# Merge-gate projections in pairs: seven products of half the size for eight, with their sums made ahead

## The chip, the cores and the metric

The kernel is one program on one core of a Trainium2 chip. The metric is device time in microseconds; before the change it is 1770.51 us, the median of 3 runs (1770.02 to 1771.18).

## What is computed

Two layers of a hybrid encoder on 512 tokens of width 1024. Each layer normalises its input to `h`, makes all queries, keys, values and gates by one projection `h @ w_in`, runs three attentions, and merges their outputs `u_a`, `u_b`, `u_m` (each already multiplied by its own gate) like this:

```python
y_a = u_a @ w_br_diff;  y_b = u_b @ w_br_dil;  y_m = u_m @ w_br_mem
gates = sigmoid(h @ w_in[:, mgate])            # 3 x 1024 columns
merged = gates[0] * y_a + gates[1] * y_b + gates[2] * y_m
x = x + merged @ w_out
```

The change touches `h @ w_in[:, mgate]`, a product of 512x1024 by 1024x3072 in each layer, and the operand of the last line.

## The kernel before

**Precision.** Every large product is made in float32r from two parts of each operand, `hi` (rounded by ScalarE, L95) and `lo = src - hi` (VectorE, L96; both in `split`, L94). `mm3` (L166) then issues three matmuls on TensorE: hi by hi (L167), hi by lo (L168), lo by hi (L169).

**Weights.** `weight_order` (L99) lists all weight units in the order of their use, most of 1024x128 (a tile of 128 partitions by 8x128). `weight` (L159) calls `prefetch` (L148), which keeps two units ahead (`LEAD`): it loads a unit from HBM on SyncE's queue into one of 3 raw buffers and splits it into one of 4 `w_hi` and one of 3 `w_lo` buffers.

**Projections.** `proj_fm` (L171) makes 128 output channels for all 512 tokens: the weight's 128x128 blocks are stationary, the transposed activations `hT_hi` and `hT_lo` (8 blocks of 128x512, made once a layer by `norm_T`, L320) move. It is 8 blocks by `mm3`, 24 matmuls of 512 columns, summed in one of four PSUM banks named `mm`.

**A layer.** First the memory keys and values and `hT`, then the attentions, which the generators in `weave` (L657) interleave, then `merge` (L580). `merge` makes 16 gated tiles `U`, read back from DRAM and split, then goes over 8 slices `d` of 128 output channels. A slice is three `proj_fm` for its gates with a sigmoid each (L601 to L603), `y` (48 matmuls with `u` moving, from the weight units `ba` and `bm`, L605 to L613), and on VectorE three products and two sums (L615 to L617) and a split into `mg_hi`, `mg_lo`. `out_proj` (L624) then holds blocks of `mg` stationary and moves `w_out` in 512 columns; it feeds the next layer's `norm_T`, or the final norm.

**Order.** Each engine works in its own order; a scheduler places instructions on the engines from the program's order and its own estimates. GpSimd (POOL) only prepares the bias tables at the start of the program.

Of the kernel before, what the change touches and what calls it, by code (L numbers as in the profile page):

```python
# [44 lines left out]
def encoder_kernel(ctx: ExitStack, tc: tile.TileContext, x, mem, g_norm, w_in, diff_lambda,  # L45
                   w_mem_kv, g_mem, w_br_diff, w_br_dil, w_br_mem, w_out, rel_bias, g_final,
                   buckets, maskrows, partrows, out):
    nc = tc.nc
# [50 lines left out]
    def weight_order():  # L99
# [19 lines left out]
        for l in range(DEPTH):  # L119
# [15 lines left out]
            for d in range(8):  # L135
                ds_ = slice(d * 128, (d + 1) * 128)
                for b in range(3):
                    yield fm(l, MGATE + b * 1024 + d * 128)
                yield ("ba", l, d), 8, 128, [(0, 8, 0, 128, w_br_diff[l, :, ds_])]
                yield ("bm", l, d), 8, 128, [(0, 4, 0, 128, w_br_mem[l, :, ds_]),  # L140
                                             (4, 8, 0, 128, w_br_dil[l, :, ds_])]
# [683 lines left out]
```

## Time and profile before

| | |
|---|---|
| median of 3 runs | 1770.51 us |
| the profiled execution | 1770.44 us, its span 1768.4 us |
| mean granted TensorE clock | 0.998 |
| busy share of the span | PE 99%, DVE 57%, ACT 47%, POOL 1% |
| matmul instructions | 9012 |
| chain that ended last | PE 97%, DMA 1%, ACT 1% |

The span is the program on the core; the 2 us over it are launch and end. PE is TensorE's matmuls, PEld its weight loads, DVE VectorE, ACT ScalarE, POOL GpSimd, SP the SyncE queue that issues most transfers. Matmuls are pipelined, so that the duration shown for one is longer than the distance to the next: what one costs a full engine is read from the starts of neighbours.

### The profile page before, as it was taken

How to read it: one execution, taken by the hardware profiler on the slowest of the kernel's cores; microseconds unless marked ns; L12 is line 12 of the kernel's file. 1: busy time of each engine (PE TensorE's matmuls, PEld its weight loads, DVE VectorE, ACT ScalarE, POOL GpSimd, SP SyncE). 2: the span in 40 equal slices, each digit the busy share in tenths (PEclk: the TensorE clock that was granted, in tenths of full speed). 3: DMA queues.
4: the chain of work that ended last, by engine and by line, in shares of the span. 5: the costliest groups of instructions: out<-in, count | busy, mean ns of one | idle time of the engine just before them, and what ended most of it. 6: DMA issues, size and time to landing. Idle time of an engine off the chain costs nothing.

```text
span 1768.4 us, 23429 instructions
## 1 busy us (share of the span) xinstructions
PE 1743.8 (99%) x9012; PEld 1496.0 (85%) x9012; DVE 1005.5 (57%) x1727; ACT 834.5 (47%) x1436; POOL 22.1 (1%) x45
## 2 busy tenths in 40 slices
PE   7999999999999999999999999999999999999998
PEld 6798889888888888888888898888988888888886
DVE  6566576666765663333465656658566747333333
ACT  6455555545555642222255555455454548322223
POOL 2200000000000000000000000000000000000000
PEclk9999999999999999999999999999999999999999
DMA  9643243332432643333572333324332336333342
GB/s 263 141 130 86 72 123 89 103 94 76 117 97 80 202 138 95 97 93 116 160 199 59 112 85 103 94 76 116 95 98 86 101 109 202 107 96 95 96 154 72
DMA packets 308847, 200.26 MB, mean 113 GB/s; under 512 B 14116, under 2 KB 283428, under 8 KB 308736
## 3 DMA queue, kind: packets, MB, share of 16 engines
q1 hardware_dynamic: 306704, 195.09, 38.3%
q0 software_dynamic: 2032, 3.68, 1.2%
q8 instruction: 71, 1.16, 0.3%
q14 instruction: 40, 0.33, 0.1%
HBM read 177.89 MB, written 20.83 MB: 112 GB/s over the span
## 4 chain that ended last, share of the span: by engine, by line
PE 97%; DMA 1%; ACT 1%; DVE 0%; issue 0%; SPq 0%; DVEq 0%; ACTq 0%
PE mm L167 27%; PE mm L169 27%; PE mm L168 27%; PE wT_ps L384 2%; PE f_s L407 2%; PE f_s L408 2%; DMA w_raw<-in_w_mem_kv 1%; PE f_o L168 1%; PE f_o L169 1%; PE f_o L167 1%; PE d_o L533 1%; PE d_s L509 1%; PE w_ps L522 0%; PE d_o L168 0%; PE d_o L169 0%; PE d_o L167 0%
## 5 line engine op out<-in xcount | busy, mean ns | idle before, releaser
L96 DVE TENSOR_TENSOR w_lo<-w_raw,w_hi 128x1024 fp32r<-128x1024 f32 (+2 forms) x296 | 335.8, 1135 | 436.1 <-PE mm L169 389.7
L95 ACT ACTIVATE w_hi<-w_raw 128x1024 fp32r<-128x1024 f32 (+2 forms) x296 | 293.3, 991 | 601.5 <-PE mm L168 296.0
L167 PE MATMUL mm<-hT_hi,w_hi 128*128 128x512 f32 x1344 | 529.9, 395 | 1.9 <-ACT hT_hi L95 1.9
L169 PE MATMUL mm<-hT_hi,w_lo 128*128 128x512 f32 x1344 | 527.3, 392 | 0.0
L168 PE MATMUL mm<-hT_lo,w_hi 128*128 128x512 f32 x1344 | 526.7, 392 | 0.0
L167 PEld LDWEIGHTS mm<-hT_hi,w_hi 128*128 128x128 f32 x1344 | 252.8, 188 | 53.2 <-ACT hT_hi L95 2.1
L169 PEld LDWEIGHTS mm<-hT_hi,w_lo 128*128 128x128 f32 x1344 | 252.9, 188 | 53.0 <-DVE w_lo L96 0.4
L168 PEld LDWEIGHTS mm<-hT_lo,w_hi 128*128 128x128 f32 x1344 | 253.0, 188 | 50.7
L169 PE MATMUL mm<-w_hi,hT_lo 128*128 128x384 f32 (+1 forms) x512 | 160.8, 315 | 0.0
L167 PE MATMUL mm<-w_hi,hT_hi 128*128 128x384 f32 (+1 forms) x512 | 160.0, 313 | 0.0
L168 PE MATMUL mm<-w_lo,hT_hi 128*128 128x384 f32 (+1 forms) x512 | 158.5, 310 | 0.0
L413 ACT ACTIVATE f_e<-f_e,f_st 128x512 f32<-128x512 f32 x128 | 91.9, 721 | 49.7 <-DVE f_st L410 49.7
L167 PE MATMUL mm<-u_hi,w_hi 128*128 128x512 f32 x256 | 101.2, 395 | 0.0
L169 PE MATMUL mm<-u_hi,w_lo 128*128 128x512 f32 x256 | 101.2, 395 | 0.0
L168 PE MATMUL mm<-u_lo,w_hi 128*128 128x512 f32 x256 | 101.1, 395 | 0.0
L167 PEld LDWEIGHTS mm<-w_hi,hT_hi 128*128 128x128 f32 x512 | 96.9, 189 | 1.0
L168 PEld LDWEIGHTS mm<-w_lo,hT_hi 128*128 128x128 f32 x512 | 96.8, 189 | 1.1
L169 PEld LDWEIGHTS mm<-w_hi,hT_lo 128*128 128x128 f32 x512 | 96.7, 189 | 0.0
L410 DVE CUSTOM_DVE_ANT_0 f_e<-f_s,f_bias 128x512 f32<-128x512 f32 x128 | 84.4, 681 | 6.8 <-PE f_s L408 6.7
L96 DVE TENSOR_TENSOR f_wTlo<-wT_ps,f_wThi 128x512 fp32r<-128x512 f32 x64 | 43.7, 683 | 31.4 <-ACT f_wThi L95 30.2
L615 DVE TENSOR_TENSOR mgate<-mm,mgate 128x512 f32<-128x512 f32 x48 | 33.0, 688 | 48.4 <-PE mm L169 48.4
L447 DVE RECIPROCAL f_sq<-f_sq 128x512 f32<-128x512 f32 x16 | 53.6, 3349 | 9.5 <-ACT f_sq L446 9.5
(203 smaller groups left out, 2403.9 us busy)
## 6 DMA issues: line engine op xcount, KB each, us to landing
w_raw<-in_w_in SPq DMA_DIRECT2D x168, 512.0 KB, 3.8
w_raw<-in_w_in SPq DMA_DIRECT2D x96, 128.0 KB, 2.4
w_raw<-in_w_mem_kv SPq DMA_DIRECT2D x16, 512.0 KB, 6.0
w_raw<-in_w_in SPq DMA_DIRECT2D x32, 256.0 KB, 2.9
u_raw<-u_d SPq DMA_DIRECT2D x32, 256.0 KB, 4.1
w_raw<-in_w_br_diff SPq DMA_DIRECT2D x16, 512.0 KB, 3.8
w_raw<-in_w_out SPq DMA_DIRECT2D x16, 512.0 KB, 3.9
f_bias<-tt_d SPq DMA_DIRECT2D x64, 112.0 KB, 4.1
```

What stands on the lines that cost most here:

```text
L95: nc.scalar.activation(hi, src, AF.Copy)
L96: nc.vector.tensor_tensor(out=lo, in0=src, in1=f32(hi), op=ALU.subtract)
L167: nc.tensor.matmul(o, lhsT=lh, rhs=rh, start=start, stop=False)
L168: nc.tensor.matmul(o, lhsT=lh, rhs=rl, start=False, stop=False)
L169: nc.tensor.matmul(o, lhsT=ll, rhs=rh, start=False, stop=stop)
L384: nc.tensor.transpose(t[:, i], s, ident)
L407: nc.tensor.matmul(sp, lhsT=qh[:, cs], rhs=K[s, m], start=True, stop=False)
L408: nc.tensor.matmul(sp, lhsT=ql[:, cs], rhs=K[s, m], start=False, stop=True)
L410: nc.vector.tensor_tensor_reduce(out=em.rearrange("p (c b) -> p c b", c=4), in0=sp, in1=bt[:, 3 - c:7 - c], op0=ALU.add, op1=ALU.min, scal ...
L413: nc.scalar.activation(em, em, AF.Exp, scale=-1.0, bias=stt[:, m:m + 1], accum_out=stt[:, 2 + m:3 + m])
L447: nc.vector.reciprocal(sq, sq)
L615: nc.vector.tensor_tensor(out=g, in0=y, in1=g, op=ALU.mult)
```

## The change

**Pairs.** In each layer 20 of the 24 merge-gate projections are done two at a time, as ten pairs; the three of slice 0 and the last of slice 7 stay as they were (`merge_steps`). Two projections of 128 channels are a product of a weight (2x2 blocks: two column groups of 128, two halves of the 1024 inputs) by `hT` (2x2 quarters: two halves of the inputs, two halves of the 512 tokens). `pair` makes it with seven products of blocks in place of eight (Winograd's form). A product is 4 blocks by `mm3`, 12 matmuls of 256 columns; 84 matmuls of 256 columns stand in place of 48 of 512.

**Left sums.** `load_pair` loads the four quarters of a pair's weights (four transfers of 256 KB in place of two of 512 KB) and makes four sums or differences of them on GpSimd, each 128x512. A pair has four weight units to split, three of 128x1024 and one of 128x512, in place of two of 128x1024.

**Right sums.** Four of the seven products have sums of quarters of `hT` as moving operand, T1 to T4. They are the same for all pairs of a layer. `right_sums` makes them with 20 VectorE instructions of 128x512 in each layer and stores them in DRAM (8 transfers of 256 KB, SyncE). The code weaves it into the attention; `right_operands` reads them back with 8 GpSimd transfers a layer and splits them during gates 7 to 15 and the unpaired projections of slice 0.

**Adding up.** The seven products of a pair are added with seven VectorE instructions and one ScalarE copy of 128x256, in the two gate tiles; the sigmoid then reads the gate tile (SBUF) and not PSUM.

**The merged slices.** They are kept as float32 (`m`), and after the last use of `hT` in the layer they are split into `hT_hi` and `hT_lo`, which `out_proj` now holds stationary in place of `mg`. `u_raw`, `u_v` and `xr` share the buffers of `m`. A smaller scratch area of the DMA rings moves all tiles to lower addresses.

```diff
+def merge_steps():
+    steps = [("one", (0, b)) for b in range(3)] + [("y", 0)]
+    for d0 in (1, 3, 5):
+        d1 = d0 + 1
+        steps += [("pair", (d0, 0), (d0, 1)), ("pair", (d0, 2), (d1, 2)), ("y", d0),
+                  ("pair", (d1, 0), (d1, 1)), ("y", d1)]
+    return steps + [("pair", (7, 0), (7, 1)), ("one", (7, 2)), ("y", 7)]
...
+    def load_pair(key):
+        l, cols = key[1], key[2:]
+        pool = pair_pool[0]
+        t1, t2, t3 = [pool.tile([128, 8, 128], F32, tag="raw", name="s_raw", bufs=4) if i < 2 else
+                      wp.tile([128, 8, 128], F32, tag="raw", name="s_raw3", bufs=3) for i in range(3)]
+        t4 = pool.tile([128, 4, 128], F32, tag="raw4", name="s_raw4", bufs=2)
+        lo, up = slice(0, 4), slice(4, 8)
+        for t, part, f, k in ((t2, lo, 1, 0), (t3, up, 1, 1), (t1, lo, 0, 0), (t3, lo, 0, 1)):
+            src = w_in[l, k * 512:(k + 1) * 512, cols[f]:cols[f] + 128]
+            dma(t[:, part], src.rearrange("(k p) n -> p k n", p=128))
+        a11, a21, a12, a22 = t1[:, lo], t2[:, lo], t3[:, lo], t3[:, up]
+        tt = nc.gpsimd.tensor_tensor
+        tt(out=t2[:, up], in0=a21, in1=a22, op=ALU.add)
+        tt(out=t1[:, up], in0=t2[:, up], in1=a11, op=ALU.subtract)
+        tt(out=a21, in0=a11, in1=a21, op=ALU.subtract)
+        tt(out=t4, in0=a12, in1=t1[:, up], op=ALU.subtract)
+        for i, t in enumerate((t1, t2, t3, t4)):
+            loaded.append((key + (i,), t))
     def prefetch(n):
-        while len(ready) < n and order:
-            key, k, cols, pieces = order.pop(0)
-            raw = wp.tile([128, k, cols], F32, tag="raw", name="w_raw", bufs=3)
-            for k0, k1, c0, c1, src in pieces:
-                dma(raw[:, k0:k1, c0:c1], src.rearrange("(k p) n -> p k n", p=128))
-            hi = wp.tile([128, k, cols], F32R, tag="hi", name="w_hi", bufs=4)
-            lo = wp.tile([128, k, cols], F32R, tag="lo", name="w_lo", bufs=3)
+        while len(ready) < n and (loaded or order):
+            if not loaded:
+                load()
+            key, raw = loaded.pop(0)
+            shape = list(raw.shape)
+            hi = wp.tile(shape, F32R, tag="hi", name="w_hi", bufs=4)
+            lo = wp.tile(shape, F32R, tag="lo", name="w_lo", bufs=3)
             split(hi, lo, raw)
             ready.append((key, hi, lo))
+        if pair_pool and len(loaded) < 3 and order and order[0][0] == "pair":
+            load()
...
+    def pair(l, colA, colB, B, gA, gB):
+        (b11, b21, b22), T = B
+        units = {}
+        def prod(u, part, rhs):
+            if u not in units:
+                units[u] = weight("pair", l, colA, colB, u)
+            (hi, lo), (rh, rl) = units[u], rhs
+            o = mm([128, S], name="s_mm")[:, 0:256]
+            for k in range(4):
+                kk = 4 * part + k
+                mm3(o, hi[:, kk], lo[:, kk], rh[:, k], rl[:, k], k == 0, k == 3)
+            return o
+        add = lambda out, x, y: nc.vector.tensor_tensor(out=out, in0=x, in1=y, op=ALU.add)
+        c11, c12, c21, c22 = gA[:, H0], gA[:, H1], gB[:, H0], gB[:, H1]
+        nc.scalar.activation(c11, prod(0, 0, b11), AF.Copy)
+        add(c12, prod(0, 1, T[1]), c11)
+        add(c21, prod(1, 0, T[2]), c12)
+        o = prod(1, 1, T[0])
+        add(c22, o, c21)
+        add(c12, o, c12)
+        add(c11, prod(2, 0, b21), c11)
+        add(c21, prod(2, 1, T[3]), c21)
+        add(c12, prod(3, 0, b22), c12)
+    H0, H1 = slice(0, 256), slice(256, 512)
+    def right_sums(pool):
+        def acc(out, x, y, op):
+            nc.vector.tensor_tensor(out=out, in0=x, in1=y, op=op)
+        for k2 in range(2):
+            def quarter(kh, ts):
+                ks = slice(4 * kh + 2 * k2, 4 * kh + 2 * k2 + 2)
+                return f32(hT_hi[:, ks, ts]), f32(hT_lo[:, ks, ts])
+            b11, b12, b21, b22 = quarter(0, H0), quarter(0, H1), quarter(1, H0), quarter(1, H1)
+            t1, t2, t3, t4 = [pool.tile([128, 2, 256], F32, tag="ts", name="t_sum", bufs=4) for _ in range(4)]
+            for t, x, y in ((t1, b12, b11), (t3, b22, b12)):
+                acc(t, x[0], y[0], ALU.subtract)
+                yield
+                acc(t, t, x[1], ALU.add)
+                yield
+                acc(t, t, y[1], ALU.subtract)
+                yield
+            for t, x, y in ((t2, b22, t1), (t4, b21, t2)):
+                acc(t, x[0], y, ALU.subtract)
+                yield
+                acc(t, t, x[1], ALU.add)
+                yield
+            for i, t in enumerate((t1, t2, t3, t4)):
+                dma(t_d[i, k2], t)
+            yield
+    def right_operands(pool):
+        T = [[pool.tile([128, 4, 256], F32R, name=f"T{i}{p}") for p in ("hi", "lo")] for i in range(4)]
+        quarter = lambda ks, ts: (hT_hi[:, ks, ts], hT_lo[:, ks, ts])
+        k1, k2 = slice(0, 4), slice(4, 8)
+        yield (quarter(k1, H0), quarter(k2, H0), quarter(k2, H1)), T
+        loads = []
+        for k2 in range(2):
+            for i in range(4):
+                t = pool.tile([128, 2, 256], F32, tag="uT", name="t_in", bufs=32)
+                pdma(t, t_d[i, k2])
+                loads.append((T[i], slice(2 * k2, 2 * k2 + 2), t))
+        yield
+        for (hi, lo), ks, t in loads:
+            split(hi[:, ks], lo[:, ks], t)
+            yield
...
     def merge(l, yu, ym, lam_init):
         U = {}
-        for i in U_ORDER:
-            raw = yu.tile([128, S], F32, tag="ul", name="u_raw", bufs=3)
+        pair_pool[:] = [yu]
+        rop = right_operands(yu)
+        B = next(rop)
+        m_tile = lambda name: ym.tile([128, S], F32, tag="m", name=name, bufs=8)
+        for n, i in enumerate(U_ORDER):
+            if n >= 7:
+                next(rop, None)
+            raw = m_tile("u_raw")
             dma(raw, u_d[i])
             if i < 8:
-                v = yu.tile([128, S], F32, tag="uv", name="u_v", bufs=3)
+                v = m_tile("u_v")
                 dma(v, v_d[i])
                 nc.scalar.activation(v, v, AF.Sqrt)
                 nc.vector.scalar_tensor_tensor(out=raw, in0=raw, scalar=1.0 - lam_init, in1=v,
...
             lo = yu.tile([128, S], F32R, tag="uT", name="u_lo", bufs=32)
             split(hi, lo, raw)
             U[i] = (hi, lo)
-        M = []
-        for d in range(8):
-            gs = []
-            for b in range(3):
+        M, G = [], {}
+        for step in merge_steps():
+            if step[0] == "pair":
+                gA, gB = [sg_tile(name="mgate") for _ in range(2)]
+                pair(l, *[MGATE + b * 1024 + d * 128 for d, b in step[1:]], B, gA, gB)
+                for db, g in zip(step[1:], (gA, gB)):
+                    nc.scalar.activation(g, g, AF.Sigmoid)
+                    G[db] = g
+                continue
+            if step[0] == "one":
+                d, b = step[1]
+                next(rop, None)
                 o = proj_fm(l, MGATE + b * 1024 + d * 128)
-                g = sg_tile(name="mgate")
-                nc.scalar.activation(g, o, AF.Sigmoid)
-                gs.append(g)
+                G[d, b] = sg_tile(name="mgate")
+                nc.scalar.activation(G[d, b], o, AF.Sigmoid)
+                if d == 7:
+                    for e, m in enumerate(M):
+                        split(hT_hi[:, e], hT_lo[:, e], m)
+                continue
+            d = step[1]
+            gs = [G.pop((d, b)) for b in range(3)]
             whi, wlo = weight("ba", l, d)
             ya = mm([128, S])
             for k in range(8):
...
             for g, y in zip(gs, (ya, yb, ym_ps)):
                 nc.vector.tensor_tensor(out=g, in0=y, in1=g, op=ALU.mult)
             nc.vector.tensor_tensor(out=gs[0], in0=gs[0], in1=gs[1], op=ALU.add)
-            nc.vector.tensor_tensor(out=gs[0], in0=gs[0], in1=gs[2], op=ALU.add)
-            hi = ym.tile([128, S], F32R, tag="mg", name="mg_hi", bufs=16)
-            lo = ym.tile([128, S], F32R, tag="mg", name="mg_lo", bufs=16)
-            split(hi, lo, gs[0])
-            M.append((hi, lo))
-        return M
-    def out_proj(l, M, done):
+            m = m_tile("m")
+            nc.vector.tensor_tensor(out=m, in0=gs[0], in1=gs[2], op=ALU.add)
+            M.append(m)
+            if d == 7:
+                split(hT_hi[:, d], hT_lo[:, d], m)
+        pair_pool[:] = []
+    def out_proj(l, done):
         for n in range(2):
             os = [mm([128, 512]) for _ in range(4)]
             for k2s in ((0,), (1,), (2, 3)):
...
                     for k2, (whi, wlo) in zip(k2s, W):
                         for k in range(2):
                             kk = 2 * k2 + k
-                            mm3(os[c], M[kk][0][:, cs], M[kk][1][:, cs], whi[:, k], wlo[:, k], kk == 0, kk == 7)
+                            mm3(os[c], hT_hi[:, kk, cs], hT_lo[:, kk, cs], whi[:, k], wlo[:, k], kk == 0, kk == 7)
                     if k2s[-1] == 3:
                         done(n, c, os[c])
...
-                fp, _ = weave((diff_proj(l, j + 1, P), 8), (dil_att(l, j, P, dp), 4))
+                gens = [(diff_proj(l, j + 1, P), 8), (dil_att(l, j, P, dp), 4)]
+                if j == 1:
+                    gens.append((right_sums(al), 22))
+                fp = weave(*gens)[0]
...
-    nc = bacc.Bacc("TRN2", target_bir_lowering=False, num_devices=1)
+    nc = bacc.Bacc("TRN2", target_bir_lowering=False, num_devices=1, dynamic_dma_scratch_size=2048)
```

Two places of the order. First VectorE where layer 0 has just completed `hT` and starts its projections. Before, only the splits of the weights and of the memory queries `m_q` and a copy for the bias tables stand there:

```order
L96 TENSOR_TENSOR hT_lo<-hT_ps,hT_hi 128x4x128 [waits Activation_49] x2
L230 COPY b_t<-b_ps 80x512 [waits PE_49]
L96 TENSOR_TENSOR w_lo<-w_raw,w_hi 128x1024 [waits DMAHW1_49,PE_49]
L458 SCALAR_TENSOR_TENSOR m_ql<-mm,m_qh 128x512 [waits Activation_49]
L96 TENSOR_TENSOR w_lo<-w_raw,w_hi 128x1024 [waits DMAHW2_49,DVE_49,PE_49]
L458 SCALAR_TENSOR_TENSOR m_ql<-mm,m_qh 128x512 [waits Activation_49]
L96 TENSOR_TENSOR w_lo<-w_raw,w_hi 128x1024 [waits DMAHW3_49,DVE_49,PE_49]
```

With the change:

```order
L259 TENSOR_TENSOR t_sum<-hT_hi 128x512 [waits DMAHW4_49]
L259 TENSOR_TENSOR t_sum<-t_sum,hT_lo 128x512 [waits DVE_49]
L259 TENSOR_TENSOR t_sum<-hT_hi 128x512 [waits DMAHW5_49]
L259 TENSOR_TENSOR t_sum<-t_sum,hT_lo 128x512 [waits DVE_49]
L107 TENSOR_TENSOR w_lo<-w_raw,w_hi 128x1024 [waits DMAHW1_49,PE_49]
L259 TENSOR_TENSOR t_sum<-t_sum,hT_lo 128x512 [waits DVE_49]
L580 SCALAR_TENSOR_TENSOR m_ql<-mm,m_qh 128x512 [waits Activation_49]
L259 TENSOR_TENSOR t_sum<-t_sum,hT_lo 128x512 [waits DVE_49]
L107 TENSOR_TENSOR w_lo<-w_raw,w_hi 128x1024 [waits DMAHW2_49,PE_49]
L259 TENSOR_TENSOR t_sum<-t_sum,hT_lo 128x512 [waits DVE_49]
L580 SCALAR_TENSOR_TENSOR m_ql<-mm,m_qh 128x512 [waits Activation_49]
L259 TENSOR_TENSOR t_sum<-hT_hi,t_sum 128x512 [waits DMAHW6_49,DVE_49]
```

The scheduler puts all 20 sums `t_sum` of a layer here and not where the code weaves them, as soon as `hT` is complete (in layer 1 at the same place); those that wait for a DMAHW semaphore need a buffer that a store to `t_d` must have left first.

Second VectorE in the merge, at the end of a slice's `y` and in what follows (`w_lo` are splits of weights, `s_raw` the units of a pair). Before:

```order
L96 TENSOR_TENSOR w_lo<-w_raw,w_hi 128x1024 [waits DVE_49,DMAHW3_49,PE_49,Activation_49]
L615 TENSOR_TENSOR mgate<-mm,mgate 128x512
L615 TENSOR_TENSOR mgate<-mm,mgate 128x512 [waits PE_49,Activation_49]
L615 TENSOR_TENSOR mgate<-mm,mgate 128x512 [waits PE_49]
L96 TENSOR_TENSOR w_lo<-w_raw,w_hi 128x1024 [waits DMAHW4_49,DVE_49,Activation_49]
L616 TENSOR_TENSOR mgate<-mgate 128x512 [waits DVE_49]
L617 TENSOR_TENSOR mgate<-mgate 128x512 [waits DVE_49]
L96 TENSOR_TENSOR mg_lo<-mgate,mg_hi 128x512 [waits Activation_49]
L96 TENSOR_TENSOR w_lo<-w_raw,w_hi 128x1024 [waits DMAHW5_49,PE_49]
```

With the change, from the start of the first pair:

```order
L242 TENSOR_TENSOR mgate<-s_mm,mgate 128x256 [waits PE_49,Activation_49]
L107 TENSOR_TENSOR w_lo<-s_raw_6198,w_hi 128x512 [waits Pool_49]
L242 TENSOR_TENSOR mgate<-s_mm,mgate 128x256 [waits DVE_49,PE_49] x2
L242 TENSOR_TENSOR mgate<-s_mm,mgate 128x256
L107 TENSOR_TENSOR w_lo<-s_raw,w_hi 128x1024 [waits Activation_49]
L242 TENSOR_TENSOR mgate<-s_mm,mgate 128x256 [waits PE_49]
L242 TENSOR_TENSOR mgate<-s_mm,mgate 128x256 [waits DVE_49,PE_49]
L107 TENSOR_TENSOR w_lo<-s_raw,w_hi 128x1024 [waits Activation_49]
L242 TENSOR_TENSOR mgate<-s_mm,mgate 128x256 [waits DVE_49,PE_49]
L107 TENSOR_TENSOR w_lo<-s_raw_6269,w_hi 128x1024 [waits DMAHW7_49,DMAHW6_49,Activation_49]
```

Between the splits there now stand the additions of the products (`s_mm`); the fourth split of a pair (128x512) waits for GpSimd's sums, and the split of the unit after next stands behind the additions of the fourth product.

## Rows read from the trace of the kernel before

**Rows 1.** The page: busy time of each engine, granted clock in 40 slices, chain by engine.
```profile
PE 1743.8 (99%) x9012; PEld 1496.0 (85%) x9012; DVE 1005.5 (57%) x1727; ACT 834.5 (47%) x1436; POOL 22.1 (1%) x45
...
PEclk9999999999999999999999999999999999999999
...
PE 97%; DMA 1%; ACT 1%; DVE 0%; issue 0%; SPq 0%; DVEq 0%; ACTq 0%
```

**Rows 2.** Windows (gates, merge): each engine's busy us (x instructions), clock, DMA share, GB/s.
```profile
560.00:633.00 73.00, 72.99 (x339) 60.46 (x337) 43.10 (x60) 46.39 (x60) 0.00 (x0) 1.00 0.56 169
633.00:854.00 221.00, 220.99 (x962) 180.44 (x963) 87.68 (x102) 64.14 (x82) 0.00 (x0) 1.00 0.37 107
```

**Rows 3.** Timeline of PE, merge: start us, duration us, engine, line; last projection, then `y`.
```profile
665.69 0.39 PE L167 MATMUL mm<-hT_hi,w_hi 128*128 128x512 f32 x1
...
670.90 0.39 PE L169 MATMUL mm<-hT_hi,w_lo 128*128 128x512 f32 x1
671.13 0.40 PE L167 MATMUL mm<-u_hi,w_hi 128*128 128x512 f32 x1
...
676.50 0.40 PE L169 MATMUL mm<-u_hi,w_lo 128*128 128x512 f32 x1
```

**Rows 4.** Timeline of PE, matmuls of 256 columns, first attention stage.
```profile
103.26 0.28 PE L167 MATMUL mm<-w_hi,hT_hi 128*128 128x256 f32 x1
...
104.92 0.28 PE L169 MATMUL mm<-w_hi,hT_lo 128*128 128x256 f32 x1
```

**Rows 5.** Timeline of PE, matmuls of 256 columns, memory keys of layer 1.
```profile
899.51 0.28 PE L167 MATMUL mm<-mT_hi,w_hi 128*128 128x256 f32 x1
...
902.22 0.28 PE L169 MATMUL mm<-mT_hi,w_lo 128*128 128x256 f32 x1
```

**Rows 6.** Timeline of PE, out projection of layer 0.
```profile
860.05 0.40 PE L169 MATMUL mm<-w_hi,mg_lo 128*128 128x512 f32 x1
...
862.85 0.40 PE L169 MATMUL mm<-w_hi,mg_lo 128*128 128x512 f32 x1
```

**Rows 7.** Groups by line and shape, PE's weight loads (busy us, mean ns).
```profile
L168 PEld LDWEIGHTS mm<-hT_lo,w_hi 128*128 128x128 f32 x1344 | 253.0, 188 | 50.7
...
L167 PEld LDWEIGHTS mm<-w_hi,hT_hi 128*128 128x128 f32 x512 | 96.9, 189 | 1.0
```

**Rows 8.** Groups by line and shape, DVE.
```profile
L96 DVE TENSOR_TENSOR w_lo<-w_raw,w_hi 128x1024 fp32r<-128x1024 f32 x232 | 283.0, 1221 | 324.6 <-PE mm L169 289.3 <-PE mm L168 22.0 <-issue 9.2
...
L615 DVE TENSOR_TENSOR mgate<-mm,mgate 128x512 f32<-128x512 f32 x48 | 33.0, 688 | 48.4 <-PE mm L169 48.4
...
L96 DVE TENSOR_TENSOR w_lo<-w_raw,w_hi 128x512 fp32r<-128x512 f32 x32 | 22.2, 693 | 61.6 <-PE mm L169 50.6 <-PE mm L168 11.0
...
L96 DVE TENSOR_TENSOR f_vlo<-mm,f_vhi 128x256 fp32r<-128x256 f32 x32 | 13.3, 420 | 3.2 <-ACT f_vhi L95 2.8
```

**Rows 9.** Timeline of DVE, start of layer 0; in brackets the idle time before and its releaser.
```profile
56.91 1.22 DVE L96 TENSOR_TENSOR w_lo<-w_raw,w_hi 128x1024 fp32r<-128x1024 f32 x1 [7.99 <-PE mm L169]
...
60.31 1.22 DVE L96 TENSOR_TENSOR w_lo<-w_raw,w_hi 128x1024 fp32r<-128x1024 f32 x1 [1.36 <-PE mm L169]
...
65.53 1.22 DVE L96 TENSOR_TENSOR w_lo<-w_raw,w_hi 128x1024 fp32r<-128x1024 f32 x1 [3.12 <-PE mm L169]
```

**Rows 10.** Timeline of DVE, start of layer 1.
```profile
929.55 1.23 DVE L96 TENSOR_TENSOR w_lo<-w_raw,w_hi 128x1024 fp32r<-128x1024 f32 x1 [2.43 <-PE mm L169]
...
935.00 1.23 DVE L96 TENSOR_TENSOR w_lo<-w_raw,w_hi 128x1024 fp32r<-128x1024 f32 x1 [3.40 <-PE mm L169]
```

**Rows 11.** Groups by line and shape, POOL.
```profile
masks.py:199 POOL TENSOR_SCALAR_AFFINE_SELECT ident<-ident 128x128 f32<-128x128 f32 x1 | 0.3, 312 | 0.1
```

**Rows 12.** DMA issues: KB each, median us to landing.
```profile
w_raw<-in_w_in SPq DMA_DIRECT2D x168, 512.0 KB, 3.8
...
w_raw<-in_w_in SPq DMA_DIRECT2D x32, 256.0 KB, 2.9
...
u_d<-o_sb SPq DMA_DIRECT2D x16, 256.0 KB, 2.1
```

More of the change, by code (lines that the diff above doesn't have):

```diff
@@ L28 @@
 LEAD = 2
-WEAVE = (0.5, -0.25)
+WEAVE = (0.5, -0.25, 0.0)
 U_COLS = [DG + i * 128 for i in range(8)] + [MG + i * 128 for i in range(4)] + [LG + i * 128 for i in range(4)]
 U_ORDER = (8, 9, 10, 11, 0, 1, 2, 3, 4, 5, 12, 13, 14, 6, 7, 15)
+def merge_steps():
[5 more added lines that the diff above has]
+    return steps + [("pair", (7, 0), (7, 1)), ("one", (7, 2)), ("y", 7)]
 def diff_v_cols(j):
@@ L82, in encoder_kernel @@
     x1_d = dr.tile([4, 128, D], F32, name="x1_d")
+    t_d = dr.tile([4, 2, 128, 2, 256], F32, name="t_d")
     memT_d = dr.tile([128, 8, NMEM], F32, name="memT_d")
@@ L134, in weight_order @@
                 yield fm(l, U_COLS[i])
-            for d in range(8):
-                ds_ = slice(d * 128, (d + 1) * 128)
-                for b in range(3):
[L138 to L141, printed above, removed]
+            for step in merge_steps():
+                if step[0] == "pair":
+                    yield ("pair", l) + tuple(MGATE + b * 1024 + d * 128 for d, b in step[1:])
+                elif step[0] == "one":
+                    yield fm(l, MGATE + step[1][1] * 1024 + step[1][0] * 128)
+                else:
+                    d = step[1]
+                    ds_ = slice(d * 128, (d + 1) * 128)
+                    yield ("ba", l, d), 8, 128, [(0, 8, 0, 128, w_br_diff[l, :, ds_])]
+                    yield ("bm", l, d), 8, 128, [(0, 4, 0, 128, w_br_mem[l, :, ds_]),
+                                                 (4, 8, 0, 128, w_br_dil[l, :, ds_])]
             for n in range(2):
@@ L145, in encoder_kernel @@
     order = list(weight_order())
-    ready = []
-    def prefetch(n):
-        while len(ready) < n and order:
-            key, k, cols, pieces = order.pop(0)
-            raw = wp.tile([128, k, cols], F32, tag="raw", name="w_raw", bufs=3)
-            for k0, k1, c0, c1, src in pieces:
-                dma(raw[:, k0:k1, c0:c1], src.rearrange("(k p) n -> p k n", p=128))
-            hi = wp.tile([128, k, cols], F32R, tag="hi", name="w_hi", bufs=4)
-            lo = wp.tile([128, k, cols], F32R, tag="lo", name="w_lo", bufs=3)
+    loaded, ready = [], []
@@ new lines, in encoder_kernel, with load @@
+    pair_pool = []
+    def load():
+        if order[0][0] == "pair":
+            load_pair(order.pop(0))
+            return
+        key, k, cols, pieces = order.pop(0)
+        raw = wp.tile([128, k, cols], F32, tag="raw", name="w_raw", bufs=3)
+        for k0, k1, c0, c1, src in pieces:
+            dma(raw[:, k0:k1, c0:c1], src.rearrange("(k p) n -> p k n", p=128))
+        loaded.append((key, raw))
+    def load_pair(key):
[16 more added lines that the diff above has]
+            loaded.append((key + (i,), t))
@@ L596, in merge @@
             U[i] = (hi, lo)
-        M = []
-        for d in range(8):
-            gs = []
-            for b in range(3):
-                o = proj_fm(l, MGATE + b * 1024 + d * 128)
-                g = sg_tile(name="mgate")
-                nc.scalar.activation(g, o, AF.Sigmoid)
-                gs.append(g)
+        M, G = [], {}
+        for step in merge_steps():
+            if step[0] == "pair":
+                gA, gB = [sg_tile(name="mgate") for _ in range(2)]
[7 more added lines that the diff above has]
+                next(rop, None)
+                o = proj_fm(l, MGATE + b * 1024 + d * 128)
+                G[d, b] = sg_tile(name="mgate")
[4 more added lines that the diff above has]
+                continue
+            d = step[1]
+            gs = [G.pop((d, b)) for b in range(3)]
             whi, wlo = weight("ba", l, d)
@@ L678, in encoder_kernel @@
     lams = []
-    M = ym_c = ym = None
+    ym_c = ym = None
     for l in range(DEPTH):
@@ L701, in done @@
                 ns = slice(n * 512, (n + 1) * 512)
-                xr = ym.tile([128, 512], F32, tag="xr", name="xr", bufs=2)
+                xr = ym.tile([128, 512], F32, tag="m", name="xr", bufs=8)
                 dma(xr, x_v[c][:, ns])
@@ L705, in done @@
                 dma(x1_d[c][:, ns], xt[c][:, ns])
-            out_proj(l - 1, M, done)
+            out_proj(l - 1, done)
             close(ym_c)
@@ L739, in encoder_kernel @@
         ym_c, ym = opened(f"ym{l}", "right")
-        M = merge(l, yu, ym, lam_init)
+        merge(l, yu, ym, lam_init)
         close(yu_c)
@@ L769, in done @@
         dma(out_v[c][:, h1], y[:, h1])
-    out_proj(DEPTH - 1, M, done)
+    out_proj(DEPTH - 1, done)
     close(ym_c)
```

## The prediction, made before the changed kernel was run

> **What bounds the kernel.** The page comes first [rows 1]: TensorE is busy 1743.8 of 1768.4 us, it holds 97% of the chain that ended last, and the granted clock is at its upper level (2.4 GHz) in all 40 slices. The windows come second [rows 2]: in the gates and in the merge of layer 0 PE is busy 72.99 of 73 and 220.99 of 221 us, DVE 43.1 and 87.7, ACT 46.4 and 64.1, POOL not at all. So the time is the sum of PE's matmuls, and a change is worth what it takes from that sum, as long as no other engine comes late. The timeline comes third, because durations of pipelined matmuls overlap: what one costs is the distance between starts. In the merge 24 matmuls with `hT` moving start between 665.69 and 670.90, 23 steps of 0.2267 us; with `u` moving, 671.13 to 676.50, 23 steps of 0.2333 [rows 3].
>
> **TensorE, removed and added.** Twenty pairs (ten a layer) remove 48 matmuls of 512 columns each: 960 x 0.2267 = 217.6 us. They add 84 of 256 columns each, 1680 in all (960 with T moving, 720 with quarters of `hT`). None of these exists before, but other matmuls of 256 columns do. From 103.26 to 104.92 are 14 steps, 0.1186 each, with `w` moving [rows 4]; from 899.51 to 902.22 are 23 steps, 0.1178 each, with `mT` moving and a weight stationary as in a pair [rows 5]. Bounds: half of 0.2267 is 0.1133; and the 6.7 ns that separate `u` from `hT`, added whole to 0.1186, give 0.1253. I take 0.1186, the slower of the two rows: 1680 x 0.1186 = 199.2 us. Balance **-18.4 us**; by the bounds -27.3 to -7.1.
>
> The out projection's 384 matmuls start 0.2333 apart (860.05 to 862.85, 12 steps) with `w` moving and `mg` stationary [rows 6]. With `hT` stationary the rows of 256 columns show no extra cost; I take 0.2267, so **-2.5 us**, with 0 as the other end.
>
> **Weight loads.** Each matmul has its own, shown as 188 ns [rows 7], more than 0.1186. That could bound a half-size product, but rows 4 and 5 carry one load of 188 ns for each matmul too and still go on every 0.118 us, so loads do not bound them. The Trainium skill ("TensorE: Matmul & The Clock Gate", What overlaps and what doesn't) says that a weight load overlaps matmuls in flight only when their row groups differ; that speaks against halving the columns, and the trace does not bear it out for these full-height matmuls. It is the rival "load" below.
>
> **VectorE in a pair.** A product is 12 x 0.1186 = 1.42 us, a pair 9.96 (before 48 x 0.2267 = 10.88). DVE makes three splits of 1.22, one of 0.69 and seven additions of 0.42 [rows 8]: 7.3 us. The tightest place is the second one shown in the order: the first unit after the pair is split behind the additions of product four. That product ends 4 x 1.42 = 5.7 us into the pair; two additions and a split (0.84 + 1.22) end at 7.7; PE wants the unit at 9.96. So **2.2 us of slack**. Over a group (three pairs, two `y`) PE takes 3 x 9.96 + 2 x 48 x 0.2333 = 52.3 us; DVE takes 3 x 7.3 and twice 2 x 1.22 + 5 x 0.69 = 5.9, together 33.7. Cost 0, covered by PE; if the cover goes, every microsecond over the slack is paid in each pair. The adds hold a PSUM bank as a sigmoid did; four banks serve products of 1.42 us, and a product is added within 2 us (0.42 behind one split of 1.22): no wait expected. ScalarE gets one and a half splits and a copy more per pair, and was idle 71% of the merge [rows 2]: 0.
>
> **GpSimd's sums.** Four per pair, of 128x512, lie ahead of the splits. The only wide row of POOL is a 128x128 operation of 312 ns [rows 11]; four times that is 1.25 us for one, and DVE's 0.69 [rows 8] is the other end. I take 1.25, so 5 us for four. Program order issues the loads one pair ahead (in `y`, or in the last `y` before two pairs in succession), landing takes 2.9 us [rows 12], so the sums end several microseconds before their splits. Cost 0. SyncE issues two more transfers per pair, of half the size; the DMA engines were 37% busy in the merge [rows 2]: 0.
>
> **The right sums.** In each layer 20 additions of 0.69 (the row of the same shape, L615) are 13.8 us of DVE, placed where `hT` is complete. In layer 0 DVE was idle 7.99 + 1.36 + 3.12 = 12.5 us there [rows 9], and layer 1 shows gaps of 2.43 and 3.40 among others [rows 10]. Four sums also wait until a store has left their buffer, 2.1 us each [rows 12], and the weight splits queue behind them: at worst 13.8 + 8.4 - 12.5 = 9.7 us late. SyncE has the stores between loads of weights. But splits run two units ahead, 2 x 5.44 - 1.22 = 9.7 us, so nearly all is hidden; between 0 and 9.7 a layer I take 0.75, near the lower end: **+1.5 us** for both. Reading back costs eight DVE and eight ACT splits, 5.5 us of DVE against 29.9 idle in the gates [rows 2], and eight transfers on POOL's queue, which is empty then: 0. The new splits into `hT` lie in the last `y` (11.2 us; seven of 0.69 are 4.8) where `mg` was split before: 0.
>
> **Sum.** 1770.4 (this execution, 0.07 under the median, so no correction) - 18.4 - 2.5 + 1.5 = **1751 us**.
>
> **Rivals.**
> *A port that DVE and POOL share.* In the merge POOL was idle before [rows 2], so no row shows the two together. If an operation of one holds the other up while it reads SBUF, DVE falls behind by up to 4p in the pair that runs while the next pair's sums are made (p is one POOL operation). That is one of the three pairs of a group, six times in the program: 6 x (4p - 2.2). At p = 1.25 it is 17 us: 1768, no difference. It decides the sign from p = 1.5, where the 19.4 us gained and the 3.5 of a difference are used up: (22.9 / 6 + 2.2) / 4. At 2.5, with two operands read at half the rate of the row, it is 47 us: **1798, slower**. For it: p is unmeasured. Against: the sums may start in `y`, where DVE is half idle, and 4p counts all four in the pair. The Trainium skill states such a lock ("SBUF — State Buffer", Who interferes with whom): an exclusive one for VectorE with two SBUF inputs against GpSimd. Its "GPSIMD Engine Reference" (section 3.1) measures 4497 ns for 2048 elements a partition; my estimate from that page is 1.1 us for 512, and by it the loss would be 13 us, 1764. Chance 0.12, two thirds of it slower.
>
> *T moves like `u`.* T1 to T4 lie in the pool of `u`, and if they or all half-size products take the 6.7 ns more, the loss is 960 or 1680 of them, 6.4 or 11.3 us, in the worst case with no gain in the out projection (2.5): 1757 to 1765, say **1761**. For: the same difference in two kinds of rows [rows 3, 6]. Against: no 256-column row has it [rows 4, 5]. Chance 0.12.
>
> *Late splits at the start of a layer.* One of the layers pays the 9.7 us worked out above: 1750 + 9.7 = **1759** (1769 with both). Against: the lead of two units. Chance 0.10.
>
> *Load.* If each half-size matmul had to wait for its weight load, 1680 x 0.188 = 316 us, 98 more than was removed: about 1868, slower. Rows 4 and 5 speak against it, the Trainium skill's rule above for it; chance 0.02.
>
> *The change saves nothing*, because a half-size matmul costs more than 4/7 of a full one: the border is 217.6 / 1680 = 0.1295, above every row here; it is counted in the second rival's tail.
>
> **Chances.** 0.64 for the forecast, 0.12, 0.12, 0.10 and 0.02 for the rivals. Low end: a pitch of 0.1167, half of 0.2333 in rows 3, makes 196.1 us, without any stall 1746. The high end, 1767, takes in the second rival, one late layer, and the milder half of the first. About 3.5 us (0.2%) can be told from no change, so faster is under 1767: 0.64 + 0.10 + 0.09 = 0.83; slower 0.08 + 0.02 = 0.10; the rest 0.07.
>
> **What would show it.** Right: 84 matmuls of 256 columns in a pair at 0.117 to 0.120 us without gaps, PE still over 98% busy, the out projection at 0.2267, DVE about 65% busy in the merge. Wrong: idle time of PE before `s_mm` released by DVE `w_lo` (the port, and then POOL's durations over 1.5 us or DVE's splits longer than 1.22), a pitch of 0.125 with T moving, or idle time of PE between 55 and 80 us released by `w_lo` behind `t_sum`.

## The result

The changed kernel takes **1754.84 us**, the median of 4 runs (1754.53 to 1756.69), beside 1770.26 for the kernel before (4 runs): a ratio of 0.9916, 95% interval 0.9904 to 0.9928. The forecast was 1751, the range 1746 to 1767. The profiled execution of the change took 1754.84, its span 1753.1. One run of the kernel with seven buffers below, of 1890.25 us at a granted clock of 0.851, was in a slower state and stays out of its median.

The page of the changed kernel (busy time, clock, chain by engine; compare [rows 1]):

```profile
PE 1724.0 (98%) x9732; PEld 1515.8 (86%) x9732; DVE 1152.4 (66%) x1963; ACT 888.9 (51%) x1516; POOL 174.0 (10%) x141
...
PEclk9999999999999999999999999999999999999999
...
PE 95%; DMA 2%; DVE 1%; ACT 1%; issue 1%; SPq 0%; ACTq 0%; DVEq 0%
```

PE has 720 matmuls more and 20 us less to do, and it is still the chain. To see where the 15 us come from, take the starts of the same matmuls in both traces; the last column is the change of each stretch (negative is gained):

```
stretch                               before            changed           difference
start to first projection of hT       0 to 47.01        0 to 46.70        -0.31
layer 0, first projection to f_s      47.01 to 118.04   46.70 to 123.47   +5.74
layer 0, attention and gates to y     118.04 to 643.57  123.47 to 648.68  -0.32
layer 0, first y to out projection    643.57 to 847.69  648.68 to 843.49  -9.31
layer 0, out projection to mT         847.69 to 892.48  843.49 to 887.05  -1.23
layer 1, mT to f_s                    892.48 to 986.87  887.05 to 981.41  -0.03
layer 1, attention and gates to y     986.87 to 1511.99 981.41 to 1507.23 +0.70
layer 1, first y to out projection    1511.99 to 1716.11 1507.23 to 1702.04 -9.31
layer 1, from the out projection on   1716.11 to 1760.67 1702.04 to 1745.37 -1.23
```

So the gain came as worked out, 9.3 us in each merge and 1.2 in each out projection, and one stretch gave 5.7 back: the projections at the start of layer 0. Layer 1, with the same 20 sums, lost nothing there. (Of its 0.70 us in the third stretch 0.56 lie between the last `f_ms` but one and the last; that was not followed up. The first stretch, which no kernel below changes, differs between them from -0.31 to +1.19 us, so a difference of 1 us between two totals says little, and the stretches say more.)

**The pair.** The timeline of PE in the changed kernel, the first pair, a product with `hT` and one with T1, and the out projection (compare [rows 3 to 6]):

```profile
659.88 0.29 PE L215 MATMUL s_mm<-hT_hi,w_hi 128*128 128x256 f32 x1
...
661.33 0.28 PE L215 MATMUL s_mm<-T1hi,w_hi 128*128 128x256 f32 x1
...
662.63 0.28 PE L217 MATMUL s_mm<-T1hi,w_lo 128*128 128x256 f32 x1
```
```profile
850.33 0.39 PE L215 MATMUL mm<-w_hi,hT_hi 128*128 128x512 f32 x1
...
853.27 0.39 PE L216 MATMUL mm<-w_lo,hT_hi 128*128 128x512 f32 x1
```

Twelve matmuls with `hT` take 1.45 us (0.1208 each), eleven steps with T1 1.30 (0.1182 each; the profile counts the four sums from T0), and the out projection goes on in 13 steps of 0.2262 where it had 0.2333. No wait of PE stands in either merge, and VectorE is busy 67% of the first (130.84 of 194.81 us). The waits of PE (released by, us in total, times, longest) hold these two:

```profile
PE mm L215 <- DVE b_t L352: 2.8, 1, 2.8
...
PE b_ps L350 <- DVE m_ql L580: 1.2, 1, 1.2
```

Neither of them is in the table of before.

**The loss.** VectorE at the start of layer 0 in the changed kernel (compare [rows 9]), and the chain that ended last in the same stretch (start, duration, what):

```profile
53.67 0.69 DVE L259 TENSOR_TENSOR t_sum<-hT_hi,t_sum 128x512 f32<-128x512 f32 x1
...
60.41 0.69 DVE L259 TENSOR_TENSOR t_sum<-hT_hi 128x512 f32<-128x512 f32 x1 [6.05 <-DMA t_d<-t_sum]
...
64.56 0.68 DVE L580 SCALAR_TENSOR_TENSOR m_ql<-mm,m_qh 128x512 fp32r<-128x512 f32 x1
...
70.56 1.28 DVE L352 COPY b_t<-b_ps 80x512 f32<-80x512 f32 x2
```
```profile
51.73 8.66 DMA t_d<-t_sum
60.41 0.76 DVE t_sum L259 x2
...
70.64 0.61 DVE b_t L352
71.29 0.80 PE mm L215
```

VectorE stands still for 6.05 us, because the layer's tenth sum needs a buffer that the first store to `t_d` must leave, and that store took 8.66 us to land. Behind it in the queue are a split of weights, the split `m_ql` of a memory query and the copies `b_t` of the bias tables. The last two hold PSUM banks: PE waits for `m_ql` (1.24 us) and then for `b_t` (2.79), 4.0 us in all. Then the granted clock is lower (windows; the third number from the right is the clock):

```profile
66.00:70.00 4.00, 1.26 (x10) 0.84 (x8) 3.96 (x6) 1.83 (x3) 0.00 (x0) 1.00 0.86 247
70.00:74.00 4.00, 2.71 (x6) 2.16 (x7) 4.00 (x7) 1.93 (x6) 2.01 (x4) 0.65 0.92 266
80.00:87.00 7.00, 7.00 (x37) 5.91 (x36) 3.80 (x5) 2.33 (x6) 1.70 (x4) 1.00 0.88 155
```

Between 67.0 and 71.3 us PE has only one matmul, of 0.27 us. Then it goes on at the lower of its two levels (1.2 GHz): the starts 71.89 to 74.02 are five steps of 0.426 us where a step is 0.2267 otherwise. Seven matmuls from 71.29 to 74.45 take 3.16 us in place of 1.59. Idle 4.03 and clock 1.57 make 5.6 of the 5.74.

**GpSimd.** Its operations are longer than the 1.25 us that I took, and they do hold VectorE up. Groups of POOL by line, then a stretch of the first layer's merge on both engines:

```profile
L189 POOL TENSOR_TENSOR s_raw<-s_raw 128x512 f32<-128x512 f32 x20 | 39.7, 1987 | 0.0
...
L188 POOL TENSOR_TENSOR s_raw<-s_raw 128x512 f32<-128x512 f32 x20 | 31.5, 1577 | 1.6
```
```profile
676.25 1.29 POOL L188 TENSOR_TENSOR s_raw<-s_raw 128x512 f32<-128x512 f32 x1
677.50 2.28 POOL L189 TENSOR_TENSOR s_raw<-s_raw 128x512 f32<-128x512 f32 x1
```
```profile
666.45 1.21 DVE L107 TENSOR_TENSOR w_lo<-s_raw,w_hi 128x1024 fp32r<-128x1024 f32 x1
...
676.42 2.20 DVE L107 TENSOR_TENSOR w_lo<-w_raw,w_hi 128x1024 fp32r<-128x1024 f32 x1
678.54 0.74 DVE L242 TENSOR_TENSOR mgate<-s_mm,mgate 128x256 f32<-128x256 f32 x2
679.21 1.65 DVE L107 TENSOR_TENSOR w_lo<-w_raw,w_hi 128x1024 fp32r<-128x1024 f32 x1
...
681.12 1.97 DVE L107 TENSOR_TENSOR w_lo<-s_raw,w_hi 128x1024 fp32r<-128x1024 f32 x1
```

Alone a GpSimd sum takes 1.29 us, and a split 1.21. The split that starts at 676.42, within the sum of 676.25, takes 2.20: it gets on when that sum ends (677.54); the next sum, from 677.50, in turn takes 2.28. One waits for the other to end, about 1.0 us at a time. The additions of the products, which read one operand from PSUM, do not grow (two in 0.74 at 678.54, while POOL works). The three splits here grow by 1.0, 0.4 and 0.8 us. PE saw none of it, for they are made ahead. The split with the least time to spare is the third of a pair, of the first unit that PE needs after the pair:

```profile
669.86 0.28 PE L215 MATMUL s_mm<-hT_hi,w_hi 128*128 128x256 f32 x1
...
679.83 0.40 PE L215 MATMUL mm<-u_hi,w_hi 128*128 128x512 f32 x1
```

Undisturbed it ends at 667.66 (the split of 666.45 above), 2.20 us before PE starts on that unit at 669.86. With the sums beside it, it ends at 678.62, 1.21 before 679.83. The least that is left in any of the twenty pairs is 1.06 us.

### The profile page after: what moved, and what is told of

The parts are those of the page before. It is cut to its first block, busy times and chain, and to the rows that moved or that the text cites. A ratio compares the mean times of both kernels' runs of the same rounds, so it can differ in the third digit from the quotient of the medians.

```text
span 1753.1 us, 25712 instructions
## 1 busy us (share of the span) xinstructions
PE 1724.0 (98%) x9732; PEld 1515.8 (86%) x9732; DVE 1152.4 (66%) x1963; ACT 888.9 (51%) x1516; POOL 174.0 (10%) x141
## 3 DMA queue, kind: packets, MB, share of 16 engines
q8 instruction: 76, 1.25, 0.3%
## 4 chain that ended last, share of the span: by engine, by line
PE 95%; DMA 2%; DVE 1%; ACT 1%; issue 1%; SPq 0%; ACTq 0%; DVEq 0%
PE mm L215 23%; PE mm L217 23%; PE mm L216 23%; PE s_mm L217 4%; PE s_mm L215 4%; PE s_mm L216 4%; PE wT_ps L506 2%; PE f_s L529 2%; PE f_s L530 2%; DMA w_raw<-in_w_mem_kv 1%; PE f_o L216 1%; PE f_o L215 1%; PE f_o L217 1%; PE d_o L655 1%; PE d_s L631 1%
## 5 line engine op out<-in xcount | busy, mean ns | idle before, releaser
L215 PE MATMUL mm<-hT_hi,w_hi 128*128 128x512 f32 x1024 | 405.7, 397 | 5.1 <-DVE b_t L352 2.8
L217 PE MATMUL mm<-hT_hi,w_lo 128*128 128x512 f32 x1024 | 403.0, 394 | 0.0
L216 PE MATMUL mm<-hT_lo,w_hi 128*128 128x512 f32 x1024 | 403.0, 394 | 0.0
L215 PEld LDWEIGHTS mm<-hT_hi,w_hi 128*128 128x128 f32 x1024 | 193.2, 189 | 45.6 <-DVE b_t L352 4.5
L217 PEld LDWEIGHTS mm<-hT_hi,w_lo 128*128 128x128 f32 x1024 | 193.0, 188 | 39.9
L217 PE MATMUL mm<-w_hi,hT_lo 128*128 128x384 f32 (+2 forms) x640 | 210.0, 330 | 0.0
L215 PE MATMUL mm<-w_hi,hT_hi 128*128 128x384 f32 (+2 forms) x640 | 209.6, 328 | 0.0
L216 PE MATMUL mm<-w_lo,hT_hi 128*128 128x384 f32 (+2 forms) x640 | 208.2, 326 | 0.0
L106 ACT ACTIVATE w_hi<-s_raw 128x1024 fp32r<-128x1024 f32 x80 | 76.1, 952 | 168.7 <-PE mm L216 105.1
L107 DVE TENSOR_TENSOR w_lo<-s_raw,w_hi 128x1024 fp32r<-128x1024 f32 x80 | 99.1, 1239 | 32.8 <-issue 32.8
```

The costliest lines, as they stand in the source:

```text
L106: nc.scalar.activation(hi, src, AF.Copy)
L107: nc.vector.tensor_tensor(out=lo, in0=src, in1=f32(hi), op=ALU.subtract)
L215: nc.tensor.matmul(o, lhsT=lh, rhs=rh, start=start, stop=False)
L216: nc.tensor.matmul(o, lhsT=lh, rhs=rl, start=False, stop=False)
L217: nc.tensor.matmul(o, lhsT=ll, rhs=rh, start=False, stop=stop)
```

## The experiments

Theory: the matmuls give what was worked out, and what is missing is one wait, of VectorE's queue for a store. Rivals: the amount of the sums is what costs; the pairs give less than they seem to; the shared access of VectorE and GpSimd costs time. Each kernel is compared with the kernel before on the same chip.

**One size: seven buffers for the sums.**

```diff
-            t1, t2, t3, t4 = [pool.tile([128, 2, 256], F32, tag="ts", name="t_sum", bufs=4) for _ in range(4)]
+            t1, t2, t3, t4 = [pool.tile([128, 2, 256], F32, tag="ts", name="t_sum", bufs=7) for _ in range(4)]
```

> The changed kernel with seven buffers for t_sum in place of four, nothing else; VectorE's order around the sums stays the same, but only one of the 20 sums of a layer still waits for a store. Theory (the wait for a store blocks VectorE's queue at the start of layer 0): the 6.05 us idle before the ninth sum goes, the copies b_t and the m_ql behind it come in time, PE's idle time of 1.24 and 2.79 us and the low clock after it go: 5.7 us less than the change, about 1749 us. Rival (the amount of the sums, 13.8 us of VectorE work in 12.5 us of idle time, is what delays): PE still waits for b_t, at least 3 us stay, 1752 to 1755.

Measured: **1748.87 us**, ratio 0.9880 (0.9863 to 0.9896). The stretch from the first projection of layer 0 to `f_s` is 1.45 us shorter than in the kernel before (it starts 1.19 later), where the change made it 5.74 longer. VectorE at the same place:

```profile
55.43 0.69 DVE L259 TENSOR_TENSOR t_sum<-hT_hi,t_sum 128x512 f32<-128x512 f32 x1
56.04 1.28 DVE L259 TENSOR_TENSOR t_sum<-hT_hi 128x512 f32<-128x512 f32 x2
...
60.18 0.69 DVE L580 SCALAR_TENSOR_TENSOR m_ql<-mm,m_qh 128x512 fp32r<-128x512 f32 x1
...
66.43 1.28 DVE L352 COPY b_t<-b_ps 80x512 f32<-80x512 f32 x2
```

The same sums in the same order, without idle time before the tenth (which the expectation calls the ninth); `b_t` comes at 66.43 and not at 70.56, and the stores still took a median of 6.8 us to land there. The rival falls: 13.8 us of sums cost PE nothing where nothing waits in between. This kernel is faster than the one before and than the change.

**The sums in the attention, where the code weaves them.**

```diff
-            nc.vector.tensor_tensor(out=out, in0=x, in1=y, op=op)
+            with tc.issue_after(mark[-1].ins):
+                nc.vector.tensor_tensor(out=out, in0=x, in1=y, op=op)
...
-                nc.vector.reciprocal(stt[:, 3:4], stt[:, 2:3])
+                mark.append(nc.vector.reciprocal(stt[:, 3:4], stt[:, 2:3]))
```

> The changed kernel with the 20 sums of a layer held behind VectorE's reciprocals of the dilated attention of j = 1, where the code weaves them. Theory: the start of layer 0 is as before the change, and the attention hides the sums: 1749 us. Rival (the sums delay wherever they stand, for VectorE feeds the softmax in the attention): PE waits for f_e there, 1750 to 1756, and layer 1, which lost nothing, now loses too.

Measured: 1753.45 us, ratio 0.9906 (0.9891 to 0.9921). The start of layer 0 is as before the change (0.17 us later at `f_s`), but between the fifth and the ninth `f_ms` each layer now loses 1.7 us. Of the waits of PE one has grown, from 2.6 us in 2 places to

```profile
PE f_ms L568 <- ACT f_sqh L106: 5.1, 4, 1.3
```

Both theories hold a part: the loss at the start is gone, and the attention does not hide the sums. The time is in the rival's range, but the wait that grew is for `f_sqh` and not for `f_e`. `f_sqh` is made from a VectorE result; that VectorE comes late to it because of the sums is likely, and was not followed further.

**No pairs, all else kept.**

```diff
-    steps = [("one", (0, b)) for b in range(3)] + [("y", 0)]
-    for d0 in (1, 3, 5):
...
+    return [s for d in range(8) for s in [("one", (d, b)) for b in range(3)] + [("y", d)]]
```

> The changed kernel with all 24 gate projections of a layer unpaired; the sums, their stores, the read-back and the out projection from hT stay. Theory (the gain is all in the pairs' matmuls, 9.2 us a layer, the out projection gives 2.5 and the start of layer 0 costs 5.7): 1770.3 + 5.7 - 2.5 = 1773.5 us. Rival (the pairs gain less, and something else in the change gains): below 1771.

Measured: 1774.64 us, ratio 1.0026 (1.0017 to 1.0036), as the theory had it (1773.5) within about 1 us. The stretches: 5.60 lost at the start, 1.23 gained in each out projection, none in the merges. So the pairs hold all the gain of the merges.

**The sums of the weights on VectorE.**

```diff
-        tt = nc.gpsimd.tensor_tensor
+        tt = nc.vector.tensor_tensor
```

> The changed kernel with the four sums of the weights on VectorE in place of GpSimd, nothing else. Theory (a GpSimd operation that meets a two-operand VectorE operation costs VectorE about 1 us, more than the 0.69 of doing it there, so nothing is lost by moving it): 1755 us within 1.5, VectorE's splits in the merge back at 1.22 us. Rival (VectorE's queue now waits for the loads and comes late in the pairs): 1758 to 1775.

Measured: 1756.13 us, ratio 0.9922 (0.9907 to 0.9936), and both merges again 9.31 us shorter than before. VectorE's groups:

```profile
L107 DVE TENSOR_TENSOR w_lo<-s_raw,w_hi 128x1024 fp32r<-128x1024 f32 x60 | 73.0, 1217 | 27.0 <-issue 22.7 <-PE mm L217 4.3
...
L187 DVE TENSOR_TENSOR s_raw<-s_raw,s_raw 128x512 f32<-128x512 f32 x20 | 13.8, 690 | 10.8 <-DMA s_raw<-in_w_in 10.7
```

With GpSimd's sums, in the change, the same splits took 1425 ns on average:

```profile
L107 DVE TENSOR_TENSOR w_lo<-s_raw,w_hi 128x1024 fp32r<-128x1024 f32 x60 | 85.5, 1425 | 32.8 <-issue 32.8
```

The theory holds. The merges are the same to 0.01 us with either engine, so moving the sums to GpSimd neither gains nor loses time there; 0.6 of the 1.3 us between this kernel and the change stand at the start of layer 0.

**Nearly twice the work on GpSimd.**

```diff
         tt(out=t2[:, up], in0=a21, in1=a22, op=ALU.add)
+        tt(out=t2[:, up], in0=a21, in1=a22, op=ALU.add)
         tt(out=t1[:, up], in0=t2[:, up], in1=a11, op=ALU.subtract)
+        tt(out=t1[:, up], in0=t2[:, up], in1=a11, op=ALU.subtract)
...
         tt(out=t4, in0=a12, in1=t1[:, up], op=ALU.subtract)
+        tt(out=t4, in0=a12, in1=t1[:, up], op=ALU.subtract)
```

> The changed kernel with three of GpSimd's four sums of every pair made twice (the repeat writes the same values), seven operations a pair in place of four. Theory (VectorE and GpSimd hold each other up, about 1.0 us per VectorE operation on two SBUF operands that meets one, and the change has slack enough for four a pair): with seven the slack of 2.2 us is used up in some pairs, PE waits for w_lo in the merge, 1757 to 1775. Rival (the slack covers seven as well, since they run in y): 1755, PE without waits in the merge.

Measured: 1758.18 us, ratio 0.9932 (0.9917 to 0.9946). The merges are 8.41 and 8.15 us shorter than before in place of 9.31, so three operations more a pair cost about 1 us a merge; the rest of the difference to the change, 1.2 us, stands before `f_s` of layer 0. (The intervals of the two ratios overlap; it is the stretches that tell the two kernels apart.) The theory holds, at the low end of its numbers. The waits that it expected are not in the list of PE's matmuls but in that of its weight loads, and in the merges of the change there are none:

```profile
PEld s_mm L220 <- DVE w_lo L107: 1.1, 4, 0.3
...
PEld s_mm L218 <- DVE mgate L245: 0.6, 3, 0.2
```

In four of the twenty pairs the third split now ends 0.41 us after PE has started on that unit: the 2.20 us are used up there, and PE waits for `w_lo`. The other three waits are for additions that free a PSUM bank. So the slack is what carries four sums and does not carry seven.

**Twelve pairs a layer (with the late sums).**

```diff
-    steps = [("one", (0, b)) for b in range(3)] + [("y", 0)]
-    for d0 in (1, 3, 5):
+    steps = []
+    for d0 in (0, 2, 4, 6):
...
-            if n >= 7:
+            if n >= 6:
                 next(rop, None)
```

> The kernel with late sums, with all 24 gate projections of a layer in 12 pairs and the read-back one gate earlier. Theory (each pair is worth 0.92 us, and the sums of the weights are made in time for the first slice too): four more pairs, 3.7 us less than with late sums, 1745 us. Rival (the first pair comes before its sums or before T1 to T4): PE waits at the start of each merge, 1747 to 1755.

Measured: **1775.11 us**, ratio 1.0022 (1.0013 to 1.0032): slower than before, a miss of 30 us. Two pairs (19.9 us) stand in front of the first `y` in place of three projections (16.3), 3.6 us more; beyond that 12 us are lost in each layer. VectorE is full there (windows; PE, PEld, DVE are the first three), and waits of PE that the change had not appear:

```profile
620.00:630.00 10.00, 8.56 (x38) 6.79 (x37) 10.00 (x7) 7.16 (x11) 8.70 (x5) 1.00 0.57 174
630.00:640.00 10.00, 5.43 (x34) 4.46 (x32) 10.00 (x17) 7.39 (x11) 0.00 (x0) 1.00 0.29 79
640.00:650.00 10.00, 7.33 (x44) 7.34 (x45) 10.00 (x16) 8.74 (x13) 0.00 (x0) 0.66 0.28 83
```
```profile
PE s_mm L217 <- DVE gate L311: 7.2, 2, 4.5
PE s_mm L219 <- DVE w_lo L107: 6.4, 2, 3.7
```
```profile
611.76 1.78 DVE L725 TENSOR_TENSOR u_raw<-u_raw,gate 128x512 f32<-128x512 f32 x1
...
615.17 2.31 DVE L107 TENSOR_TENSOR w_lo<-w_raw,w_hi 128x1024 fp32r<-128x1024 f32 x1
617.40 0.68 DVE L725 TENSOR_TENSOR u_raw<-u_raw,gate 128x512 f32<-128x512 f32 x1
```

The first pair's sums fall into the last gates, where VectorE has two-operand work on SBUF without gaps: `u_raw`, 0.69 us, takes 1.78, and a split 2.31. After the pause PE again runs at the lower level (0.66 in the third window). A full VectorE alone is not the cause: in the change it is as full from 620 to 640 (10.00 in both windows), and PE loses nothing there, with projections and not pairs behind the gates.

**Twelve pairs, with the sums of the weights on VectorE.**

```diff
-        tt = nc.gpsimd.tensor_tensor
+        tt = nc.vector.tensor_tensor
```

> The kernel with late sums and 12 pairs a layer, with the sums of the weights on VectorE in place of GpSimd. Theory (what made 12 pairs slow is that GpSimd's sums hold VectorE up in the gates): without it VectorE has only 2.8 us more work per pair there, most of the 20 us lost at the two merge starts comes back, 1749 to 1760. Rival (VectorE has simply too much to do there with four splits and T1 to T4): it stays at 1772 or more.

Measured: 1765.47 us, ratio 0.9973 (0.9962 to 0.9984), between the two theories. The loss in front of the first `y` falls from 12.2 and 12.0 us to 7.6 and 8.1. So the meeting of the two engines made some 4 us a layer of it. In the larger part that is left, PE's one long wait in each layer is for ScalarE's copy of the first product, and in front of it ScalarE (9.94 of 10 us) is as full as VectorE (10.00):

```profile
PE s_mm L217 <- ACT mgate L246: 10.6, 2, 5.3
```
```profile
620.00:630.00 10.00, 10.00 (x50) 8.44 (x49) 10.00 (x16) 9.94 (x15) 0.00 (x0) 1.00 0.41 120
```

From 600 to 640 us ScalarE makes 11 table loads of 1.28 us, as it changes between square root and sigmoid in the gates. So the amount of work is the likely rest: four splits, T1 to T4 and the last gates in one stretch, which the unpaired first slice keeps apart. Which of the two engines sets it was not tried.

**Eleven pairs a layer, seven buffers.**

```diff
-    steps = [("one", (0, b)) for b in range(3)] + [("y", 0)]
-    for d0 in (1, 3, 5):
+    steps = [("one", (0, 0)), ("one", (0, 1)), ("pair", (0, 2), (1, 2)), ("y", 0), ("pair", (1, 0), (1, 1)), ("y", 1)]
+    for d0 in (2, 4, 6):
...
-            if n >= 7:
+            if n >= 6:
                 next(rop, None)
```

> The kernel with seven buffers for t_sum, with the third projection of slice 0 paired with that of slice 1 and those of the last slices paired too: 11 pairs a layer, two unpaired projections at the start of the merge, the read-back one gate earlier. Theory (the stall with 12 pairs comes from GpSimd's sums falling into the gates, where VectorE is nearly full): most of it stays, since the sums of the first pair still fall into the last gates, 1752 to 1762. Rival (two unpaired projections, 10.9 us, are enough distance): two pairs more by 0.92 each, 1747 us.

Measured: 1750.43 us, ratio 0.9889 (0.9874 to 0.9904), not to be told from ten pairs with seven buffers. Neither expectation held: the time lies between the two. Two more pairs should give 1.8 us, yet from the last `f_ms` to the out projection the layers are 0.7 and 0.95 us longer than with ten pairs; PE waits 2.1 us for `w_lo` in 2 places that the seven buffers alone did not have. That is the theory's direction at less than its price.

## Why the prediction was right, and where it was off

- **Which engine bounds, and the pitch of a half-size matmul: right.** 0.1186 was taken, 0.118 to 0.121 came, and the merges gave 18.6 us where 18.4 was worked out. The rivals "load" and "T moves like `u`" are out: one weight load of 188 ns goes with each matmul in the pairs too, and T1 is the faster of the two operands.
- **The out projection: right**, 2.46 us for 2.5.
- **The 2.2 us of slack in VectorE's queue: right.** 2.20 us where no sum of GpSimd meets the split, and no wait of PE in a merge.
- **The shared port: right as a mechanism, wrong as a price.** The rows of POOL and DVE above show VectorE's splits (two operands in SBUF) and GpSimd's sums each waiting for the other to end. That agrees with the Trainium skill ("SBUF — State Buffer", Who interferes with whom), which states an exclusive lock. GpSimd's 1.58 to 1.99 us are above the border of 1.5 that the rival gave, and by its formula, 6 x (4 x 1.8 - 2.2), 30 us were to be lost; none were. The formula charged VectorE with GpSimd's whole duration; an operation that meets one grows by 1.0. It also took one pair of three to be hit, and in the trace sums fall into two of three, twelve pairs in the program. What counts is the growth of the one split that carries the slack, at most 1.1 us, so 1.06 were left; that the price would be so small was not worked out beforehand. My estimate from the Trainium skill's "GPSIMD Engine Reference" (section 3.1), 1.1 us for one operation, is a little under the 1.29 us that one takes alone here.
- **The right sums: the term that was mis-sized.** "+1.5 us for both" was taken, between 0 and 9.7 a layer; measured are 5.7 in layer 0 and 0 in layer 1. Two steps failed. The store was taken at 2.1 us to land, from another store's row; here 16 stores took 2.0 to 8.7, the longest where it was waited for. And the cover was the lead of the weight splits, but what came late was not a split of weights: it was `m_ql` and `b_t`, which have no lead and hold PSUM banks. The clock's fall after the pause, 1.6 us, was not counted at all. The rival "late splits" was nearest, with the right place, time (5.7 of 9.7 us) and queue, and the wrong instruction.
- **The sum.** 1770.4 less 18.6 and 2.5, plus 5.7, is 1755.0; with no loss at the start it is 1749.3, and the kernel with seven buffers took 1748.87.

Open: why that store took 8.7 us. In the windows the DMA engines were 89% busy from 54 to 58 us, and four transfers of the bias tables, of 192 KB, were on their way since 50.2; layer 1 has no such transfers, and VectorE waited 0.85 us there. That these delay the store was not tried by itself.
